# A two-layer hybrid block and two attention layers on one core: two weights of the next stage loaded into other pools, head norms in two halves

## The chip, the core and the metric

The kernel runs on one core of a Trainium2 chip. The metric is the device time of one execution in microseconds, as the median of several runs. TensorE does the matrix products, VectorE and ScalarE the elementwise work, GpSimd small steps on scale factors, and SyncE's queue issues the transfers from and to HBM.

## The reference, cut

512 tokens of 1024 channels, float32. A first block has two layers; each computes, with RMS norms over the channels:

```python
for l in range(DEPTH):                       # 2
    h = rms_norm(x, pre_mix_g[l]);  z = h @ w_in[l]
    mix = concat([o_a, o_b, o_c, o_d]) @ w_out[l]
    x = x + rms_norm(mix, post_mix_g[l])
    h = rms_norm(x, pre_ffn_g[l])
    y = conv_glu_ffn(h, ffn_w_gate[l], ffn_w_up[l], ffn_conv_w[l], ffn_w_down[l])
    x = x + rms_norm(y, post_ffn_g[l])
```

The four mixers of a layer, 256 channels each, are HGRN2 (a), gated linear attention (b), latent attention (c) and a gated delta net (d). In a, b and d each head of 64 channels of the output is RMS-normed and multiplied by a gate: these are the head norms. The FFN has 2816 inner channels. Behind this block come a layer A (differential attention) and a layer B (stick-breaking attention), both with attention to a memory of 256 rows, which the change doesn't touch in the source.

## The kernel before

**Products.** Float32 operands are split into a high and a low part of the type that TensorE takes (float32r), and a product is three matmuls: high by high, high by low, low by high (`mm3`). For a weight of 128 x 1024, `wload` (line 799) transfers it to a tile of pool "wr", ScalarE casts it into a tile of "wh" (the high part), and VectorE subtracts that from the original into a tile of "wl" (the low part). `preload` (790) does this ahead of need and keeps the result; the next `wload` of the same weight takes it. Pool "wr" has 2 tiles, "wh" and "wl" 4 each. The other large tiles (`p4`, 128 x 1024 or two halves) come from the pools "h" (8 tiles), "p" (8) and "w" (16). PSUM has the pools psA (3), psS (3) and psD (2).

**Stages.** Tokens go in four token tiles of 128. Each of the four stages of the first block (mixers 0, FFN 0, mixers 1, FFN 1) ends with `out_proj` (1829): 4 (mixers) or 11 (FFN) pairs of row blocks of the output weight, for two halves of 512 output channels. The last four pairs of the second half are held back, so that their products finish one token tile after another. For each tile, `residual_norm` (1793, the `done` in the code) squares the two halves (ScalarE), makes the scale (GpSimd: multiply and add, then a power), multiplies by it and by the gain (VectorE) and adds to the residual (VectorE); then `next_norm` (850) norms the tile for the next stage (square on ScalarE, scale on GpSimd, multiplication on VectorE), and `trans_split` (839) transposes it on TensorE and splits it into high (ScalarE) and low (VectorE) parts of h, two token tiles later. `rest()` transposes the last two tiles. `fm_first` (879) starts the next stage with three weights on the first 256 tokens, then calls `rest()`, then does the other 256. Only at the last token tile does `out_proj` call `preload(*then)` for the next stage's first weights. The squares and scaled halves stand in tiles of pool "p" behind the mixers and of "w" behind the FFN.

**Head norms.** `finish` (1044) norms the heads of the mixers a, b and d of each layer, six calls: square over 1024 columns (four token tiles of 256), sums over 64 columns, then the scale of 16 columns on GpSimd (`rstd`, 742: multiply and add, then a power), the multiplication by the gate, and that by the scale.

**Order.** Nothing is issued when it is written. The class `Plan` (262) records every operation, and all of them are issued by line 328. `feasible` (378) ranks them under the capacity of the pools, `simulate` (422) runs a list scheduler with its own costs over the five queues, and `order` (410) returns the order of the whole program. A change of one tile's pool or of one operation's size can so move any instruction of the program; each engine then takes its own queue strictly in order and waits at its head.

## Time and profile before

| | us |
|---|---|
| runs | 2032.98, 2035.56, 2035.82 |
| median | 2035.56 |
| the profiled execution's own time | 2033.99 |
| its span | 2032.2 |
| TensorE busy in it | 1954.1 (96%) |
| VectorE busy | 1250.3 (62%) |
| ScalarE busy | 946.6 (47%) |
| GpSimd busy | 265.7 (13%) |

The chain of work that ended last consists of TensorE for 84% of the span, VectorE for 7%, ScalarE for 3% and GpSimd for 2%. The stages can be told by what TensorE multiplies: mixers 0 until 325 us, a first seam until 376, FFN 0 until 710, a second seam until 745, mixers 1 until 1050, a third seam until 1100, FFN 1 until 1434, a fourth seam until 1475, layer A until 1740, layer B until the end. The table by stage shows where TensorE stands still, and the rows of single engines in the seams and in the mixers what it stands still for. As all operations are issued from one line, rows are told apart by their tiles: wr, wh and wl are a weight, its high and its low part; p4h is h; p4w and p4p are tiles of the pools "w" and "p"; st are small tiles with sums and scale factors.

### The profile page before, as it was taken

To read this page: it belongs to the slowest core of one execution; us is meant where nothing else is said; L and a number is where in the kernel's file an instruction comes from. 1 tells how busy PE (TensorE), PEld (TensorE's weight loads), DVE (VectorE), ACT (ScalarE), POOL (GpSimd) and SP (SyncE) were. 2 spreads that over 40 slices of the span, in tenths; PEclk is the share of its full clock that TensorE was granted. 3 is DMA by queue.
4 is the path that set the end of the run, shared out by engine and by line. 5 is a ranking of instruction groups with operands and counts; after the bars stand their busy time and mean duration, and the time that the engine had idled before them with its cause. 6 is when DMAs were issued, how large, how long until landed. Compare 5 with 4: busy or idle time off the path is not lost.

```text
span 2032.2 us, 33173 instructions
## 1 busy us (share of the span) xinstructions
PE 1954.1 (96%) x13254; PEld 1655.6 (81%) x13254; DVE 1250.3 (62%) x2319; ACT 946.6 (47%) x1715; POOL 265.7 (13%) x362
## 2 busy tenths in 40 slices
PE   7999989899999989998898999999999999999999
PEld 6888778788888878887787888888899988888787
DVE  7688873544442257878836444422548886558796
ACT  5744463433332236633634333322446774457782
POOL 3101111000000021011201000000223220005131
PEclk9999989999999999999999999999999999999999
DMA  5321224433332433302243333324331213421121
GB/s 166 97 63 36 83 81 138 125 94 94 98 99 94 155 90 96 92 24 68 82 152 112 100 94 94 99 97 167 121 89 43 84 63 114 135 84 55 60 74 62
DMA packets 231305, 191.62 MB, mean 94 GB/s; under 512 B 22352, under 2 KB 201200, under 8 KB 231152
## 3 DMA queue, kind: packets, MB, share of 16 engines
q1 hardware_dynamic: 231152, 189.51, 30.4%
q8 instruction: 104, 1.70, 0.3%
q14 instruction: 49, 0.40, 0.1%
HBM read 174.28 MB, written 15.20 MB: 93 GB/s over the span
## 4 chain that ended last, share of the span: by engine, by line
PE 84%; DVE 7%; ACT 3%; POOL 2%; issue 2%; DMA 1%; SPq 1%; DVEq 0%; ACTq 0%; POOLq 0%
PE psA L328 63%; PE psS L328 12%; PE psD L328 9%; DVE p4w L328 5%; POOL st L328 2%; ACT p4w L328 1%; DVE p4p L328 1%; DVE wl L328 1%; SPq L328 1%; DVE p L328 1%; ACT wh L328 0%; DMA wr<-in_w_in_dram 0%; ACT p4p L328 0%; ACT p L328 0%; DVE p4h L328 0%
## 5 line engine op out<-in xcount | busy, mean ns | idle before, releaser
L328 PE MATMUL psA<-p4h,wh 128*128 128x512 f32 (+1 forms) x2144 | 627.9, 377 | 14.3 <-DVE p4h L328 7.1
L328 DVE TENSOR_TENSOR wl<-wr,wh 128x1024 fp32r<-128x1024 f32 (+6 forms) x304 | 349.0, 1152 | 413.7 <-ACT wh L328 408.4
L328 ACT CAST wh<-wr 128x1024 fp32r<-128x1024 f32 (+6 forms) x304 | 298.5, 990 | 465.2 <-PE psA L328 279.8
L328 PEld LDWEIGHTS psA<-p4h,wh 128*128 128x128 f32 x2144 | 393.5, 191 | 89.9 <-DVE p4h L328 8.3
L328 PE MATMUL psA<-p4h,wl 128*128 128x512 f32 (+1 forms) x1072 | 400.6, 374 | 0.0
L328 PE MATMUL psA<-wh,p4h 128*128 128x256 f32 (+1 forms) x1792 | 353.8, 289 | 0.9 <-DVE p4h L328 0.7
L328 PEld LDWEIGHTS psA<-wh,p4h 128*128 128x128 f32 x1792 | 282.3, 188 | 6.6 <-issue 2.0
L328 PE MATMUL psA<-wl,p4h 128*128 128x256 f32 (+1 forms) x896 | 257.5, 288 | 0.4 <-DVE wl L328 0.4
L328 PEld LDWEIGHTS psA<-p4h,wl 128*128 128x128 f32 x1072 | 204.3, 191 | 37.0
L328 POOL TENSOR_SCALAR st<-st 128x1 f32<-128x1 f32 (+4 forms) x108 | 46.1, 427 | 1310.6 <-ACT p4w L328 908.5
L328 PEld LDWEIGHTS psA<-wl,p4h 128*128 128x128 f32 x896 | 168.8, 188 | 2.6 <-DVE wl L328 0.8
L328 PE MATMUL psA<-wh,p4w 128*128 128x512 f32 (+1 forms) x540 | 159.4, 368 | 0.0
L328 ACT ACTIVATE p<-p 128x512 f32<-128x512 f32 (+2 forms) x174 | 87.3, 526 | 100.2 <-DVE p L328 98.9
L328 POOL TENSOR_TENSOR st<-st,c 128x1 f32<-128x1 f32 (+4 forms) x106 | 115.4, 1090 | 8.0
L328 ACT ACTIVATE p4w<-psA 128x256 f32<-128x256 f32 (+5 forms) x138 | 61.6, 452 | 107.0 <-PE psA L328 105.9
L328 PEld LDWEIGHTS psA<-wh,p4w 128*128 128x128 f32 x540 | 96.6, 188 | 18.2 <-issue 0.5
L328 PE MATMUL psS<-consts,p4w 128*128 128x128 f32 (+1 forms) x448 | 70.5, 291 | 36.7 <-DVE p4w L328 28.9
L328 PE MATMUL psS<-p4w,p4w 128*64 128x64 f32 (+9 forms) x800 | 94.6, 271 | 5.3 <-DVE p4w L328 5.1
L328 PE MATMUL psA<-wl,p4w 128*128 128x512 f32 (+1 forms) x270 | 98.5, 365 | 0.0
L328 PE MATMUL psS<-wh,p4w 128*128 128x512 f32 x300 | 97.3, 395 | 0.0
L328 DVE TENSOR_TENSOR p<-psA,p 128x512 f32<-128x512 f32 x54 | 37.3, 691 | 95.8 <-PE psA L328 94.2
L328 PEld LDWEIGHTS psS<-consts,p4w 128*128 128x128 f32 x448 | 54.5, 153 | 47.7 <-issue 19.1
(227 smaller groups left out, 3105.0 us busy)
## 6 DMA issues: line engine op xcount, KB each, us to landing
wr<-in_w_in_dram SPq DMA_DIRECT2D x44, 512.0 KB, 3.8
wr<-in_ffn_w_gate_dram SPq DMA_DIRECT2D x44, 512.0 KB, 3.8
wr<-in_ffn_w_up_dram SPq DMA_DIRECT2D x44, 512.0 KB, 3.8
wr<-in_ffn_w_down_dram SPq DMA_DIRECT2D x44, 512.0 KB, 3.5
wr<-in_w_out_dram SPq DMA_DIRECT2D x16, 512.0 KB, 4.7
wr<-in_a_w_in_dram SPq DMA_DIRECT2D x16, 512.0 KB, 3.8
wr<-in_b_w_in_dram SPq DMA_DIRECT2D x16, 512.0 KB, 3.9
p4w<-xd SPq DMA_DIRECT2D x12, 512.0 KB, 4.4
```

The costliest lines, as they stand in the source:

```text
L328: op.fn(*op.args, **op.kw)
```

## The change

`out_proj` takes a string `early`. Ahead of the loop over the last products it preloads the first two weights of the next stage, the first into two tiles (high and low) of pool "p", the second into two of pool "w". All four callers give "pw". The weights that `then` names beyond these two are preloaded at the last token tile as before. `finish` does the sums, the scale and the two multiplications in two halves of 512 columns (two token tiles, 8 scale factors each). The unused argument `eng` goes.

```diff
@@ -787,16 +787,16 @@
         self.mm(ps, a, b[0], True, False)
         self.mm(ps, a, b[1], False, not more)
 
-    def preload(self, *views, eng=None):
+    def preload(self, *views, tag=None):
 
         for v in views:
             if self.wkey(v) not in self.ready_w:
-                self.ready_w[self.wkey(v)] = self.wload(v, eng)
+                self.ready_w[self.wkey(v)] = self.wload(v, tag)
 
     def wkey(self, view):
         return view.tensor.name, view.offset, tuple(view.shape)
 
-    def wload(self, view, eng=None):
+    def wload(self, view, tag=None):
 
         if self.wkey(view) in self.ready_w:
             return self.ready_w.pop(self.wkey(view))
@@ -805,10 +805,13 @@
         for k in range(sh[1] if len(sh) == 4 else 1):
             part = (slice(None), k) if len(sh) == 4 else slice(None)
             self.SP.dma_start(out=raw[part], in_=view[part])
-        hi = self.new(self.pwh, 4, sh, F32R, "wh", "wh")
-        lo = self.new(self.pwl, 4, sh, F32R, "wl", "wl")
+        if tag:
+            hi, lo = (self.p4(sh, F32R, tag) for _ in range(2))
+        else:
+            hi = self.new(self.pwh, 4, sh, F32R, "wh", "wh")
+            lo = self.new(self.pwl, 4, sh, F32R, "wl", "wl")
         self.A.copy(hi, raw)
-        self.sub(lo, raw, hi.bitcast(F32), eng)
+        self.sub(lo, raw, hi.bitcast(F32))
         return hi, lo
 
     def mm3(self, out, a, b, start, stop):
@@ -1044,15 +1047,18 @@
     def finish(self, o, gate, kt0, pst):
 
         sq = self.p4()
-        self.act(sq, o, AF.Square)
         ss = self.st([128, 16])
-        self.rsum(ss, sq.rearrange("p (a d) -> p a d", d=64))
+        parts = [(slice(i * 512, i * 512 + 512), slice(i * 8, i * 8 + 8)) for i in range(2)]
+        heads = lambda a: a.rearrange("p (a d) -> p a d", d=64)
+        for c, n in parts:
+            self.act(sq[:, c], o[:, c], AF.Square)
+            self.rsum(ss[:, n], heads(sq[:, c]))
         yield lambda: gate.get("done")
-        r = self.rstd(ss, 64)
-        self.mul(o, o, gate["gate"])
-        yield self.when(r)
-        ov = o.rearrange("p (a d) -> p a d", d=64)
-        self.mul(ov, ov, r.unsqueeze(2).broadcast_to([128, 16, 64]))
+        for c, n in parts:
+            r = self.rstd(ss[:, n], 64)
+            self.mul(o[:, c], o[:, c], gate["gate"][:, c])
+            yield self.when(r)
+            self.mul(heads(o[:, c]), heads(o[:, c]), r.unsqueeze(2).broadcast_to([128, 8, 64]))
         yield self.when(o)
         self.to_mixT(o.rearrange("p (t c) -> p t c", t=NT), kt0, pst, gate["gain"])
 
@@ -1826,7 +1832,7 @@
                 yield 0.0
         return views, gen
 
-    def out_proj(self, W, lhs, order, done, first, second, then):
+    def out_proj(self, W, lhs, order, done, first, second, then, early=""):
 
 
 
@@ -1853,6 +1859,8 @@
                 ps1 = [self.ps(p) for p in second]
             for t in range(NT):
                 part(ps0 if i < len(order) else ps1, t, n, w)
+        for v, tag in zip(then, early):
+            self.preload(v, tag=tag)
         for t in range(NT):
             if not late:
                 ps1[t] = self.ps(second[t])
@@ -1899,7 +1907,7 @@
         self.xt = self.load_x(acts[NF - 1][:, 0, :].bitcast(F32), "w")
         return self.out_proj(Wd, lambda k, t: (acts[k][:, 0, t * 128:(t + 1) * 128], acts[k][:, 1, t * 128:(t + 1) * 128]),
                              list(range(0, NF, 2)), lambda t, ps: self.residual_norm(t, ps, gb, "w"),
-                             "SSSD", "AAAD", then)
+                             "SSSD", "AAAD", then, "pw")
 
     def layer1(self, l, steps):
 
@@ -1923,7 +1931,7 @@
         self.xt = self.load_x(mt[3][:, 0, :].bitcast(F32), "p")
         steps = self.out_proj(Wo, lambda k, t: (mt[k][:, 0, t * 128:(t + 1) * 128], mt[k][:, 1, t * 128:(t + 1) * 128]),
                               order, lambda t, ps: self.residual_norm(t, ps, gb, "p"), "AAAD", "SSSD",
-                              self.ffn_views(l)[:3])
+                              self.ffn_views(l)[:3], "pw")
         if self.upto == f"mix{l}":
             return run(steps)
         h, rest = self.next_norm(steps, I["pre_ffn_g"][l], "h")
```

The order in which the instructions stand shows where the moved ones come to stand. VectorE at seam 1 (mixers 0 to FFN 0), from the low half of h of token tile 0 on, before. wl_767 and wl_770 are the first two weights of the FFN, p4w_758 the normed token tile 2, p4p_775 the scaled halves of tile 3, p4p_691 its residual, and the last row is the low half of h of tile 1:

```order
L328 TENSOR_TENSOR p4h_700<-psS_763,p4h_696 128x2x128
L328 TENSOR_TENSOR wl_767<-wr_765,wh_766 128x1024
L328 SCALAR_TENSOR_TENSOR p4w_758<-p4p_690,st_761,p4w_692 128x1024
L328 TENSOR_TENSOR wl_770<-wr_768,wh_769 128x1024
L328 SCALAR_TENSOR_TENSOR p4p_775<-psD_704,st_778,p4w_687 128x512
L328 SCALAR_TENSOR_TENSOR p4p_775<-psD_764,st_778,p4w_687 128x512
L328 TENSOR_TENSOR p4p_691<-p4p_691,p4p_775 128x512 x2
L328 TENSOR_TENSOR p4h_697<-psS_784,p4h_693 128x2x128
```

VectorE at the same place after the change. p4p_737 and p4w_740 are the low parts of the first two weights, wl_779 is that of the third, p4w_770 the normed tile 2, p4p_781 the scaled halves of tile 3, and p4h_703 ends the piece with the low half of tile 1. Its first part, at the residual of tile 0:

```order
L328 TENSOR_TENSOR wl_734<-wr_732,wh_733 128x1024
L328 TENSOR_TENSOR p4p_737<-wr_735,p4p_736 128x1024
L328 SCALAR_TENSOR_TENSOR p4p_743<-psA_707,st_746,p4w_693 128x512
L328 SCALAR_TENSOR_TENSOR p4p_743<-psS_741,st_746,p4w_693 128x512
L328 TENSOR_TENSOR p4w_740<-wr_738,p4w_739 128x1024
L328 TENSOR_TENSOR p4p_694<-p4p_694,p4p_743 128x512 x2
```

and VectorE in its second part, at the end of the seam:

```order
L328 TENSOR_TENSOR p4h_706<-psS_775,p4h_702 128x2x128
L328 TENSOR_TENSOR wl_779<-wr_777,wh_778 128x1024
L328 SCALAR_TENSOR_TENSOR p4w_770<-p4p_696,st_773,p4w_698 128x1024
L328 SCALAR_TENSOR_TENSOR p4p_781<-psD_710,st_784,p4w_693 128x512
L328 SCALAR_TENSOR_TENSOR p4p_781<-psD_776,st_784,p4w_693 128x512
L328 TENSOR_TENSOR p4p_697<-p4p_697,p4p_781 128x512 x2
L328 TENSOR_TENSOR p4h_703<-psS_790,p4h_699 128x2x128
```

The subtractions of the first two weights moved up to the residual of tile 0; that of the third stands where that of the first stood, and none stands between the norm of tile 2 and the residual of tile 3.

VectorE at seam 2 (FFN 0 to mixers 1) before, from the low half of tile 0 on. wl_1158 and wl_1161 are the first two weights of the mixers, p4w_1150 the normed tile 2, p4w_1163 the scaled halves of tile 3, p4w_1008 its residual, and p4h_1049 the low half of tile 1:

```order
L328 TENSOR_TENSOR p4h_1052<-psS_1155,p4h_1048 128x2x128
L328 TENSOR_TENSOR wl_1158<-wr_1156,wh_1157 128x1024
L328 TENSOR_TENSOR wl_1161<-wr_1159,wh_1160 128x1024
L328 SCALAR_TENSOR_TENSOR p4w_1150<-p4w_1007,st_1153,p4w_1044 128x1024
L328 SCALAR_TENSOR_TENSOR p4w_1163<-psD_1056,st_1166,p4w_1004 128x512
L328 SCALAR_TENSOR_TENSOR p4w_1163<-psD_1096,st_1166,p4w_1004 128x512
L328 TENSOR_TENSOR p4w_1008<-p4w_1008,p4w_1163 128x512 x2
L328 TENSOR_TENSOR p4h_1049<-psS_1172,p4h_1045 128x2x128
```

VectorE at seam 2 after the change. wl_1182 is the small weight of the mixers, cast and subtracted in pieces, wl_1196 the next full weight, p4w_1152 and p4w_1162 are the normed tiles 1 and 2, and p4h_1055 is the low half of tile 1:

```order
L328 TENSOR_TENSOR p4h_1058<-psS_1167,p4h_1054 128x2x128
L328 TENSOR_TENSOR wl_1182<-wr_1180,wh_1181 128x8x56
L328 TENSOR_TENSOR wl_1182<-wr_1180,wh_1181 128x8x8
L328 TENSOR_TENSOR wl_1182<-wr_1180,wh_1181 128x8x32
L328 TENSOR_TENSOR wl_1182<-wr_1180,wh_1181 128x8x16 x2
L328 TENSOR_TENSOR wl_1196<-wr_1194,wh_1195 128x1024
L328 SCALAR_TENSOR_TENSOR p4w_1152<-p4w_1012,st_1155,p4w_1050 128x1024
L328 SCALAR_TENSOR_TENSOR p4w_1162<-p4w_1013,st_1165,p4w_1050 128x1024
L328 SCALAR_TENSOR_TENSOR p4w_1169<-psD_1062,st_1172,p4w_1010 128x512
L328 SCALAR_TENSOR_TENSOR p4w_1169<-psD_1102,st_1172,p4w_1010 128x512
L328 TENSOR_TENSOR p4w_1014<-p4w_1014,p4w_1169 128x512 x2
L328 TENSOR_TENSOR p4h_1055<-psS_1178,p4h_1051 128x2x128
```

The two full subtractions left (they stand above, beside the residuals); the small weight and one full weight came in, and the norm of tile 1 moved down behind them.

VectorE at the tail of mixers 0 before. p4w_495 is the output of the last of the head-normed mixers, st_651 its scale of 16 columns; p4w_645 and p4w_658 are the normed rows of the memory attention:

```order
L328 TENSOR_TENSOR p4w_495<-p4w_495,p4p_289 128x1024
L328 TENSOR_SCALAR st_634<-st_633 128x1
L328 TENSOR_TENSOR p4w_495<-p4w_495,st_651 128x1024
L328 SCALAR_TENSOR_TENSOR p4w_645<-p4w_646,st_649,p4w_640 128x1024
L328 SCALAR_TENSOR_TENSOR p4w_658<-p4w_659,st_662,p4w_640 128x1024
```

VectorE there after the change (p4w_650 and p4w_664 are the memory rows, st_656 and st_661 the two scales of 8 columns):

```order
L328 SCALAR_TENSOR_TENSOR p4w_650<-p4w_651,st_654,p4w_645 128x1024
L328 TENSOR_SCALAR p_544_639<-p_544_639,st_640 128x512
L328 SCALAR_TENSOR_TENSOR p4w_664<-p4w_665,st_668,p4w_645 128x1024
L328 COPY p4w_632<-psD_657 128x2x128
L328 TENSOR_TENSOR p4w_495<-p4w_495,p4p_289 128x512 x2
L328 TENSOR_TENSOR p4w_495<-p4w_495,st_656 128x512
L328 TENSOR_TENSOR p4w_495<-p4w_495,st_661 128x512
```

The memory rows moved ahead of the multiplications by gate and scale, which now stand in halves.

## Rows read from the trace of the kernel before

**Rows 1.** Table by stage; columns: us, PE, PEld, DVE, ACT, POOL busy (xcount), PEclk, DMA, GB/s.

```profile
0.00:325.00 325.00, 296.21 (x2968) 253.00 (x2969) 245.80 (x519) 170.42 (x310) 52.84 (x69) 0.98 0.33 97
325.00:376.00 51.00, 43.86 (x231) 36.91 (x230) 27.12 (x40) 20.34 (x46) 11.18 (x20) 0.93 0.32 107
376.00:710.00 334.00, 334.00 (x1485) 273.60 (x1486) 137.21 (x159) 107.65 (x135) 0.58 (x3) 1.00 0.35 106
710.00:745.00 35.00, 28.09 (x129) 22.68 (x128) 21.23 (x34) 15.38 (x37) 11.15 (x19) 0.91 0.31 98
...
1434.00:1475.00 41.00, 39.65 (x237) 33.94 (x237) 28.74 (x45) 19.45 (x44) 12.64 (x25) 1.00 0.35 116
```

**Rows 2.** TensorE's timeline at seam 1: start, us, engine, line, op, [idle before <-releaser].

```profile
357.05 0.51 PE L328 MATMUL psA<-p4h,wh 128*128 128x256 f32 x2 [0.64 <-ACT p4h L328]
359.59 0.63 PE L328 MATMUL psS<-consts,p4w 128*128 128x128 f32 x4 [2.04 <-DVE p4w L328]
363.49 0.58 PE L328 MATMUL psA<-p4h,wh 128*128 128x256 f32 x1 [3.27 <-DVE p4h L328]
```

**Rows 3.** VectorE's timeline at seam 1.

```profile
350.62 1.30 DVE L328 SCALAR_TENSOR_TENSOR p4w<-p4p,st,p4w 128x1024 f32<-128x1024 f32 x1 [2.19 <-POOL st L328]
...
356.21 1.21 DVE L328 TENSOR_TENSOR wl<-wr,wh 128x1024 fp32r<-128x1024 f32 x1
358.15 1.30 DVE L328 SCALAR_TENSOR_TENSOR p4w<-p4p,st,p4w 128x1024 f32<-128x1024 f32 x1 [0.72 <-POOL st L328]
359.37 1.21 DVE L328 TENSOR_TENSOR wl<-wr,wh 128x1024 fp32r<-128x1024 f32 x1
360.50 1.40 DVE L328 SCALAR_TENSOR_TENSOR p4p<-psD,st,p4w 128x512 f32<-128x512 f32 x2
...
363.02 0.74 DVE L328 TENSOR_TENSOR p4h<-psS,p4h 128x256 fp32r<-128x256 f32 x2
```

**Rows 4.** GpSimd's timeline at seam 1.

```profile
349.75 0.19 POOL L328 TENSOR_SCALAR st<-st 128x1 f32<-128x1 f32 x1 [3.97 <-ACT p4w L328]
...
356.24 1.24 POOL L328 TENSOR_SCALAR st<-st 128x1 f32<-128x1 f32 x1 [3.91 <-ACT p4w L328]
```

**Rows 5.** TensorE's timeline at seam 2.

```profile
739.79 1.08 PE L328 MATMUL psS<-consts,p4w 128*128 128x128 f32 x4 [3.65 <-DVE p4w L328]
742.91 0.80 PE L328 MATMUL psA<-p4h,wh 128*128 128x256 f32 x2 [2.04 <-ACT wh L328]
```

**Rows 6.** Timeline of VectorE and GpSimd at seam 2.

```profile
734.29 2.35 DVE L328 TENSOR_TENSOR wl<-wr,wh 128x1024 fp32r<-128x1024 f32 x2
734.38 2.39 POOL L328 TENSOR_SCALAR st<-st,st 128x1 f32<-128x1 f32 x1 [3.42 <-ACT p4w L328]
...
738.36 1.28 DVE L328 SCALAR_TENSOR_TENSOR p4w<-p4w,st,p4w 128x1024 f32<-128x1024 f32 x1 [1.72 <-POOL st L328]
```

**Rows 7.** TensorE's timeline at seam 4.

```profile
1465.50 0.50 PE L328 MATMUL psA<-wh,p4h 128*128 128x256 f32 x2 [0.75 <-DVE p4h L328]
```

**Rows 8.** Timeline of the start: GpSimd, VectorE, TensorE.

```profile
10.21 0.56 POOL L328 TENSOR_TENSOR st<-st,c 128x1 f32<-128x1 f32 x1
...
11.00 1.23 DVE L328 TENSOR_TENSOR wl<-wr,wh 128x1024 fp32r<-128x1024 f32 x1 [2.62 <-ACT wh L328]
...
13.47 1.12 PE L328 MATMUL psS<-consts,p4w 128*128 128x128 f32 x4 [3.08 <-DVE p4w L328]
```

**Rows 9.** VectorE's timeline at the tail of mixers 0.

```profile
286.30 1.29 DVE L328 SCALAR_TENSOR_TENSOR p4w<-p4w,st,p4w 128x1024 f32<-128x1024 f32 x1 [0.73 <-POOL st L328]
```

**Rows 10.** Groups by line and form, whole span: xcount, busy us, mean ns, idle before.

```profile
L328 DVE TENSOR_TENSOR p4w<-p4w,p4p 128x1024 f32<-128x1024 f32 x10 | 12.2, 1217 | 0.0
...
L328 DVE TENSOR_TENSOR p4w<-p4w,p4w 128x512 f32<-128x512 f32 x16 | 10.3, 682 | 0.0
...
L328 POOL TENSOR_TENSOR st<-st,c 128x16 f32<-128x16 f32 x10 | 32.9, 3285 | 0.8
...
L328 POOL TENSOR_TENSOR st<-st,c 128x8 f32<-128x8 f32 x12 | 21.9, 1827 | 1.0
```

## The prediction

> **What bounds the kernel now.** I read the table by stage first [rows 1]. TensorE is busy for 334.00 of the 334 us of the first FFN stage and for 296.21 of the mixers' 325 us, at a granted clock of 1.00 and 0.98: there the time is TensorE's own work, and the change takes no product away. The seams between the stages are the exception. Seam 1 (first mixers to first FFN, 325 to 376 us) leaves TensorE idle for 51.00 - 43.86 = 7.1 us at a clock of 0.93, seam 2 (first FFN to second mixers, 710 to 745 us) for 35.00 - 28.09 = 6.9 us at 0.91, seam 3 (second mixers to second FFN) repeats seam 1, and seam 4 (second FFN to layer A) for only 41.00 - 39.65 = 1.35 us at 1.00. So some 7.1 + 6.9 + 7 + 1.35 = 22 us of the 2032 are idle in the four places that the change speaks of.
>
> Then TensorE's own rows at seam 1 [rows 2]: it waits 0.64, 2.04 and 3.27 us, and the longest wait ends when VectorE has written the low half of h for token tile 1; products run without a gap only from 363.49. Why that half is late stands in VectorE's rows [rows 3]: a weight's subtraction (1.21 us from 356.21), the norm of token tile 2 (from 358.15, after 0.72 us of waiting for GpSimd), another subtraction (1.21 us from 359.37), two residual products and two additions, and only then, at 363.02, the split that TensorE needs. GpSimd's rows [rows 4] tell why the norm waits: its scale step ends late because a step on 128x1, which took 0.19 us at 349.75, took 1.24 from 356.24, while VectorE's subtraction ran.
>
> Seam 2 shows it larger [rows 5, 6]: TensorE waits 3.65 and 2.04 us; two subtractions run for 2.35 us from 734.29, and GpSimd's step on 128x1 takes 2.39 us beside them. The norm that TensorE waits for starts at 738.36. Seam 4 is nearly full already: the longest wait there is 0.75 us [rows 7].
>
> **Part 1, the two early weights.** No instruction is added: two loads, two casts and two subtractions of a seam go earlier, into tiles of other pools. What counts is what stands ahead of the split in VectorE's queue afterwards, and the change's order tells that. At seam 1 the two subtractions go up beside the residuals of token tiles 0 and 1, where VectorE has gaps (2.19 us ahead of 350.62, while from 358.15 on it has none) [rows 3]. But the third weight's subtraction takes the place of the first ahead of the norm of tile 2, and the split of tile 1 still stands behind that norm and behind the residual of tile 3. So one subtraction slot leaves: 1.21 us as a row, about 1.13 as the distance to the next start (359.37 to 360.50). Against it, the two weight tiles take two of the pool "p" slots in which the residuals' squares are made, so that the square of tile 2 waits for an earlier addition; I charge 0.1 us. Gain 1.0 us at seam 1, and 1.0 at seam 3, whose waits are the same. Bounds of each: a loss of 0.5 (the moved subtractions push the additions ahead of the squares by part of their 1.21) to a gain of 2.4 (the slot, plus GpSimd's step back from 1.24 to 0.19, which frees the norm by 1.05, and some of the wait behind it).
>
> A page of the Trainium skill, "SBUF — State Buffer", section "Who interferes with whom", says that a VectorE instruction with two SBUF inputs and a GpSimd instruction that reads SBUF exclude each other for a whole instruction. The traces agree: the step of 128x1 lasts as long as the two subtractions beside it [rows 6]. By the page alone, taking both subtractions out of the place would give the whole GpSimd stretch back (rival B); by the order, another subtraction stands in the same place, and the sum keeps 1.0.
>
> At seam 2 the two subtractions (2.35 us) leave as well, but in the change's order the small-weight subtractions (five of them) and one of the next full weight now stand ahead of the norms of tiles 1 and 2; the norm of tile 1 stood ahead before. 2.35 - 1.21 for the full weight [rows 3] leaves 1.1; for the small ones, of which the trace of before shows none in this place, I take 0.3, between nothing and the 1.2 of a full weight, nearer to nothing since they hold 448 of 1024 columns. That is 0.8, with bounds of a loss of 1.5 (the third weight's load lands late and both norms wait behind it) and a gain of 2.5. At seam 4 no more than the 1.3 us of idle time can go; I take 0.5 (0 to 1.3). The seams give 1.0 + 1.0 + 0.8 + 0.5 = 3.3 us.
>
> **Part 2, the head norms in halves.** In each of six places a full pass over 1024 columns becomes two over 512: the multiply by the gate 1217 to 2 x 682 ns, the multiply by the scale and the sum likewise [rows 10]. That is 0.15 us more for each of the three, 0.45 on VectorE; on GpSimd the power of 16 columns at 3285 ns becomes two of 8 at 1827, so 0.37 us more. ScalarE's square becomes two as well; ScalarE is busy for 170.42 of the 325 us [rows 1], and I charge nothing. The first half of the scale factors is ready about 1.5 us sooner, the second 0.4 later. These norms stand in the mixers, where TensorE has other products to run (296.21 of 325 busy), so I cost them at nothing where they stand as before; without that cover they cost 6 x (0.45 + 0.37) = 4.9 us, which is rival D.
>
> A page of the Trainium skill, "VectorE: DVE Perf Modes", section "The TRN2 errata — SBUF-src ops pay a fixed extra latency per instruction", speaks against this part: each instruction pays a fixed extra cost, many small tiles pay it each. The rows agree, 2 x 682 against 1217 ns. By the page's 58 cycles at 0.96 GHz it would be an estimated 0.06 us per instruction more, by the rows 0.15; the rows decide.
>
> **What moves with it.** The scheduler lays out the whole program anew, so three other places change. At the start, the norm of token tile 1 now goes ahead of the first weight's subtraction on VectorE; before, the subtraction ran from 11.00 for 1.23 us and the norm behind it, and TensorE waited 3.08 us for that norm until 13.47 [rows 8]. Its scale is ready when GpSimd's power ends, at 10.21 + 0.56 = 10.77, so that the norm can start near 10.9, 1.2 sooner. The next wait, for the h of tile 0 and its weight, then ends later by the same subtraction: I take 0.8 of gain (0 to 1.3). At the tail of the mixers the norms of the memory rows stood behind the two multiplies of the last head norm (1.2 us each, as the group of the first says [rows 10]) and then waited 0.73 us each for GpSimd (one of the two waits is in [rows 9]); they now stand ahead of the halves. The two 0.73 can go and nothing else by it, half of it at both tails: 0.75 each, 1.5 in all (bounds: a loss of 1, since the head norm's transposes come later, to a gain of 3 each). Everywhere else I take zero, and 5 us either way as a bound: the first mixers leave TensorE idle for 325 - 296.21 = 28.8 us, start included [rows 1], the second for about half of that, and a new order may shift a ninth of the sum.
>
> **The sum.** 3.3 + 0.8 + 1.5 = 5.6 us off. The profiled execution took 2033.99 us (span 2032.2 and 1.8 around it): 2028.4. The median of three runs is 2035.56, 1.6 above the profiled one, so on its scale 2030.0. A change of 0.2% is 4.1 us, about what a measurement of this kernel tells from none: faster is below 2031.5, slower above 2039.6.
>
> **The rivals.** B, the seams give all: neither the third weight's subtraction nor the small ones collide with GpSimd, so that each of seams 1 to 3 gives 2.4 us (2.35 at seam 2 [rows 6], the upper bound above at the others). 7.2 + 0.5 + 0.8 + 1.5 = 10.0: about 2025.6. For it speak the rows of GpSimd [rows 4, 6]; against it the order, in which another subtraction takes the place. 0.20. C, the seams give nothing: the split of tile 1 still stands behind the norm of tile 2 and the residual of tile 3 in VectorE's queue, and the chain from the last product through the square, GpSimd and the residual is as long as before; the saved slot is then only waiting. With the start's 0.8 alone: 2034.8. For it speaks that the split stands where it stood; against, that VectorE was busy without a gap from 358.15 to 363.02, with the subtraction among it [rows 3]. 0.21. D, slower: the head norms' halves lie on the path. VectorE takes its queue in order; where the second half's scale ends last and the multiply by it stands ahead of work that TensorE waits for, each of six places costs 0.45 + 0.37 = 0.82, and 4.9 with nothing gained at the seams gives 2035.6 + 4.9 = 2040.5. It decides where the second multiply stands within some 2 us of the first, less than GpSimd's 1827 ns and its first step behind one another. For it: all three multiplies stand in one row in the change's order; against: TensorE has other work in most of those places. The reshuffle's 5 us of loss would end there too. 0.17. A, the forecast, 0.42.
>
> **How the numbers follow.** A reaches over 2026 to 2034, B over 2022 to 2028, C over 2032 to 2038, D from 2039.6 on. Leaving out most of D and the last of B, 2022 to 2040 holds 8 in 10. Faster by over 0.2%: all of B and seven tenths of A, 0.50. Within: the rest of A and C, 0.33. Slower: 0.17.
>
> **What would show it.** Seam 1's products without a gap from about 362.4 instead of 363.49 after the last output product, and seam 2's from a time 0.8 earlier against its last output product: Part 1 holds. A step on 128x1 of GpSimd at 0.2 us in both seams, and a norm of tile 2 a microsecond sooner: B. The same distance as before from the last output product to the first dense one: C. Waits of VectorE for GpSimd ahead of the second halves, with TensorE waiting for VectorE behind them: D. A mixer stage that takes 3 us more or less than 325 or 305 would say that the new order outside the seams counts for more than all of these, and that would make the prediction wrong in its reasons even where the time is right.

## The result, and the profile after

The changed kernel takes 2025.28 us (median of five runs, 2023.03 to 2030.09) against 2035.82 (five runs, 2032.98 to 2037.69): a ratio of 0.9950, with a 95% interval of 0.9933 to 0.9967. In a second comparison (the run after_again below) the ratio was 0.9933 (0.9919 to 0.9946). One of the 29 runs of before in it took 2162.66 us at a granted clock of 0.843 and is left out of the ratio. So it is faster by 10 to 14 us; 2030.0 was forecast, with 2022 to 2040 as the range. The time came out on that of rival B (2025.6), but not by B's mechanism.

The profiled execution of the changed kernel took 2030.09 us (span 2027.9), the slowest of its five runs. Its table by stage, with the columns and the cuts of [rows 1]:

```profile
0.00:325.00 325.00, 296.27 (x2954) 254.91 (x2955) 246.03 (x528) 168.73 (x312) 52.67 (x73) 0.96 0.32 94
325.00:376.00 51.00, 46.04 (x237) 39.09 (x236) 28.80 (x39) 20.47 (x43) 9.17 (x20) 0.93 0.41 133
376.00:710.00 334.00, 333.63 (x1488) 273.59 (x1487) 136.37 (x160) 107.11 (x138) 0.58 (x3) 1.00 0.33 103
710.00:745.00 35.00, 31.11 (x139) 25.17 (x138) 23.73 (x40) 17.64 (x39) 9.72 (x17) 0.91 0.47 142
...
1434.00:1475.00 41.00, 41.00 (x264) 36.86 (x263) 28.15 (x43) 18.67 (x44) 15.85 (x29) 1.00 0.45 142
```

TensorE is busier in the seams (46.04 of 51 us instead of 43.86, 31.11 of 35 instead of 28.09, all of 41 instead of 39.65), but the cuts of before fall at other places of the work here. A closer measure is the distance from the last output product of a seam to the first product of the next stage behind which TensorE stands still no more. TensorE's timeline at seam 1, of before and then of after; the last output product is the first row of each:

```profile
354.13 0.40 PE L328 MATMUL psD<-wh,p4w 128*128 128x512 f32 x1
...
355.78 0.63 PE L328 MATMUL psS<-consts,p4w 128*128 128x128 f32 x4 [0.81 <-DVE p4h L328]
```

```profile
357.46 0.40 PE L328 MATMUL psD<-wh,p4w 128*128 128x512 f32 x1
...
359.11 0.39 PE L328 MATMUL psA<-p4h,p4p 128*128 128x256 f32 x1 [0.38 <-ACT p4h L328]
...
361.64 0.63 PE L328 MATMUL psS<-consts,p4w 128*128 128x128 f32 x4 [1.91 <-DVE p4w L328]
364.94 1.43 PE L328 MATMUL psA<-p4h,p4p 128*128 128x256 f32 x5 [2.67 <-DVE p4h L328]
```

Before it is 363.49 [rows 2] - 354.13 = 9.36 us, after 364.94 - 357.46 = 7.48. The waits are 0.38, 1.91 and 2.67 us, where [rows 2] have 0.64, 2.04 and 3.27, and the one of 0.81 went. Here are the same distances and the pieces between them for the profiled executions that the argument goes by (us; each is worked out from two such rows; "rest" runs from the last product of FFN 1 to the end of the span):

| kernel | mixers 0 | seam 1 | FFN 0 | seam 2 | mixers 1 | seam 3 | FFN 1 | rest | span |
|---|---|---|---|---|---|---|---|---|---|
| before | 354.1 | 9.36 | 369.7 | 9.77 | 335.1 | 9.29 | 369.6 | 575.3 | 2032.2 |
| before_again | 353.1 | 9.36 | 369.4 | 9.79 | 337.7 | 9.29 | 369.8 | 575.8 | 2034.3 |
| after | 357.5 | 7.48 | 370.2 | 5.96 | 335.9 | 7.48 | 370.5 | 573.0 | 2027.9 |
| after_again | 350.8 | 7.48 | 369.9 | 5.96 | 332.2 | 7.48 | 370.4 | 573.3 | 2017.4 |
| early_only | 358.1 | 7.47 | 370.5 | 7.81 | 335.5 | 7.53 | 370.0 | 573.6 | 2030.5 |
| halves_only | 351.5 | 9.33 | 370.8 | 9.78 | 337.8 | 9.32 | 370.5 | 576.1 | 2035.0 |
| halves_again | 350.4 | 9.35 | 370.8 | 9.79 | 336.7 | 9.36 | 369.5 | 574.7 | 2030.5 |
| squares_first | 354.1 | 7.68 | 370.4 | 9.64 | 336.2 | 7.67 | 370.3 | 581.0 | 2037.0 |
| no_low_parts | 353.2 | 8.22 | 370.2 | 6.36 | 335.5 | 8.15 | 370.2 | 576.1 | 2027.8 |

Two things are to be read in it. The seams repeat to 0.04 us between two executions of one kernel, so one profile is enough for them. The mixers do not: they differ by 6.7 us (357.5 and 350.8) between two executions of the changed kernel alone.

One thing the table hides: the distance ends where TensorE stands still no more, and how much it has multiplied by then differs from kernel to kernel. Counted in the same timelines to the start of the tenth product of the next stage, ahead of which every kernel here has done the same twelve transposes, the distances are (us):

| kernel | seam 1 | seam 2 | seam 3 |
|---|---|---|---|
| before, before_again | 11.02, 11.02 | 11.43, 11.45 | 10.95, 10.95 |
| after, after_again | 8.92, 8.93 | 9.26, 9.26 | 8.93, 8.93 |
| early_only | 8.91 | 9.26 | 8.98 |
| halves_only, halves_again | 10.99, 11.02 | 11.43, 11.45 | 10.98, 11.02 |
| squares_first | 9.34 | 11.31 | 9.33 |
| no_low_parts | 9.67 | 7.52 | 9.60 |

By equal work the seams gave 2.1, 2.2 and 2.0 us, 6.3 in all. At seam 2 the first table shows 3.8, because in the changed kernel the gapless stretch begins with less work done.

The mean of the two executions after less that of the two before is 2022.65 - 2033.25 = -10.6 us; by the pieces of the first table: the three seams -7.5, the rest (seam 4 with layers A and B) -2.4, mixers 1 -2.4, mixers 0 +0.5, and the FFNs +1.2. That last goes with the clock. At seam 1, in the 3 us behind the first 3 us of gapless products the granted clock was 0.93 before and 0.67 after, so a part of the idle time that TensorE saved was spent again at 1.2 GHz.

```profile
366.50:369.50 3.00, 3.00 (x26) 3.00 (x26) 2.20 (x4) 0.00 (x0) 0.00 (x0) 0.93 0.55 161
```

```profile
367.90:370.90 3.00, 3.00 (x19) 3.00 (x19) 2.40 (x3) 0.00 (x0) 0.00 (x0) 0.67 0.09 24
```

### The profile page after: what moved, and what is told of

It is laid out like the page before. It is cut to its first block, busy times and chain, and to the rows that moved or that the text cites. A ratio compares the mean times of both kernels' runs of the same rounds, so it can differ in the third digit from the quotient of the medians.

```text
span 2027.9 us, 33217 instructions
## 1 busy us (share of the span) xinstructions
PE 1959.3 (97%) x13254; PEld 1664.9 (82%) x13254; DVE 1252.7 (62%) x2337; ACT 943.5 (47%) x1719; POOL 261.0 (13%) x374
## 4 chain that ended last, share of the span: by engine, by line
PE 82%; DVE 8%; ACT 2%; issue 2%; DMA 2%; POOL 2%; SPq 1%; DVEq 0%; ACTq 0%; POOLq 0%
PE psA L328 62%; PE psS L328 12%; PE psD L328 9%; DVE p4w L328 5%; POOL st L328 2%; ACT p4w L328 1%; DVE p4p L328 1%; DVE st L328 1%; DVE wl L328 1%; SPq L328 1%; DVE p L328 1%; DMA dn<-p4w 1%; ACT wh L328 0%; DVE p4h L328 0%; DMA p4p<-in_x_dram 0%
## 5 line engine op out<-in xcount | busy, mean ns | idle before, releaser
L328 DVE TENSOR_TENSOR wl<-wr,wh 128x1024 fp32r<-128x1024 f32 (+4 forms) x296 | 339.4, 1151 | 413.3 <-ACT wh L328 408.1
L328 PE MATMUL psA<-p4h,wh 128*128 128x512 f32 (+1 forms) x1952 | 588.5, 384 | 0.0
L328 ACT CAST wh<-wr 128x1024 fp32r<-128x1024 f32 (+4 forms) x296 | 290.0, 989 | 480.3 <-PE psA L328 285.4
L328 PEld LDWEIGHTS psA<-p4h,wh 128*128 128x128 f32 x1952 | 362.5, 190 | 76.4 <-issue 2.5
L328 PE MATMUL psA<-p4h,wl 128*128 128x512 f32 (+1 forms) x976 | 376.2, 386 | 0.0
L328 PE MATMUL psA<-wh,p4h 128*128 128x256 f32 (+1 forms) x1728 | 345.9, 291 | 0.0
L328 PEld LDWEIGHTS psA<-wh,p4h 128*128 128x128 f32 x1728 | 275.2, 189 | 4.9 <-issue 2.0
L328 PE MATMUL psA<-wl,p4h 128*128 128x256 f32 (+1 forms) x864 | 249.9, 290 | 0.0
L328 PEld LDWEIGHTS psA<-p4h,wl 128*128 128x128 f32 x976 | 185.7, 190 | 33.1
L328 POOL TENSOR_SCALAR st<-st 128x1 f32<-128x1 f32 (+4 forms) x114 | 39.7, 348 | 1274.0 <-ACT p4w L328 872.4
```

The source lines that it names most:

```text
L328: op.fn(*op.args, **op.kw)
```

## The experiments

My theory after the first profile: the seams give the gain, each by its own queue. Rivals: the halves and the order that they bring give it; or any new order of the whole program does.

**The two parts apart.** after_again is the changed kernel itself. early_only has `finish` as before; halves_only has `out_proj` and its callers as before; early_mix_only is early_only with one caller fewer:

```diff
-                             "SSSD", "AAAD", then, "pw")
+                             "SSSD", "AAAD", then)
```

> The changed kernel once more, for a second profile. Its five runs reached from 2023.0 to 2030.1 us and the profiled one was the slowest of them. Theory (the seams give the gain): the distance from the last output product to the first gapless product of the next stage is again 7.5 us at seams 1 and 3 (before 9.4 and 9.3) and about 6 at seam 2 (before 9.8), whatever the run's time; the median lies at 2023 to 2028. Rival (the new order inside the mixers gives the gain and the seams little): the end of the first mixers' output products, at 357.5 us in the first profile against 354.1 before, moves ahead of 354 in a run of 2025 or less.

> The early weights alone, the head norms whole as before. Theory (seams): 1.9 + 3.8 + 1.8 us at seams 1 to 3, some 1 to 2 at the start and at seam 4, so 8 to 10 off: 2026 to 2028. Rival (the halves and the order that they bring give it): 2 to 4 off, 2032 to 2034.

> The head norms in halves alone, all weights of the next stage preloaded at the last token tile as before. Theory (seams): no change or a small one, 2033 to 2037, with the distances at the seams as before (9.4, 9.8, 9.3). Rival (halves give the gain): 2026 to 2030. Rival D of the prediction (the halves lie on the path): 2039 to 2041.

> The early weights only where the mixers end (seams 1 and 3), not where the FFNs end; the head norms whole. Theory (each seam gives its own part): 1.9 + 1.8 us at the two seams and what the start gives, so 3.5 to 5 off: 2031 to 2032.5, the distance at seam 2 as before (9.8). Rival (the order of the whole program gives the gain): a time that has nothing to do with the two seams, off by over 3 us from this.

All four were compared with the same runs of before (median 2036.75). after_again: 2022.59, ratio 0.9933 (0.9919 to 0.9946). early_only: 2033.15, ratio 0.9984 (0.9976 to 0.9993). halves_only: 2033.05, ratio 0.9988 (0.9976 to 0.9999). early_mix_only: 2032.81, ratio 0.9982 (0.9969 to 0.9995). So each part alone is worth 0.1 to 0.2%, and both together 0.7%: more than the sum of the two. The seams belong to the early weights alone (early_only has 7.47, 7.81, 7.53; halves_only 9.33, 9.78, 9.32; by the tenth product early_only has all of the changed kernel's gain at each seam), as the theory says; but early_only missed the 2026 to 2028 expected of it, and halves_only, at 2033.05, lies at the edge of "no change". Where the rest of the gain comes from is told below, with the clock.

early_mix_only (2031 to 2032.5 expected, so a little above) shows 7.48 at seam 1 and, as expected, 9.77 at seam 2, where nothing is early; but at seam 3, 10.56 us instead of 7.5. That seam is told below, with w_after_ffn.

**What shortened seams 1 and 3.** The prediction had put it down to a subtraction slot that leaves VectorE's queue. The trace of after doesn't bear this out. ScalarE's timeline at seam 1, before:

```profile
348.52 1.06 ACT L328 ACTIVATE p4w<-p4p 128x1024 f32<-128x1024 f32 x1 [4.88 <-DVE p4p L328]
...
349.57 0.58 ACT L328 ACTIVATE p4p<-psS 128x512 f32<-128x512 f32 x1
```

and after:

```profile
351.42 0.60 ACT L328 ACTIVATE p4p<-psS 128x512 f32<-128x512 f32 x1 [0.54 <-PE psS L328]
...
352.01 1.05 ACT L328 ACTIVATE p4w<-p4p 128x1024 f32<-128x1024 f32 x1
```

The square over 128x512 from psS is that of the residual of token tile 2, the square over 128x1024 the norm square of tile 1. Before, the first stands behind the second, which waits 4.88 us for VectorE; after, it stands ahead. Two rows of VectorE are swapped with them: the norm of tile 1 stood ahead of the scaled halves of tile 2 (350.62 [rows 3], then 352.36) and now stands behind them (354.55, behind 353.22). GpSimd's power for these halves ran beside that norm before and doesn't any more. GpSimd before, and after:

```profile
350.93 1.40 POOL L328 TENSOR_TENSOR st<-st,c 128x1 f32<-128x1 f32 x1
```

```profile
352.63 0.55 POOL L328 TENSOR_TENSOR st<-st,c 128x1 f32<-128x1 f32 x1
```

Counted from the last output product, VectorE began the norm of tile 2 at 358.15 [rows 3] - 354.13 = 4.02 us before and at 360.20 - 357.46 = 2.74 after. VectorE at seam 1 after, from the last subtraction ahead of the split:

```profile
358.27 1.22 DVE L328 TENSOR_TENSOR wl<-wr,wh 128x1024 fp32r<-128x1024 f32 x1
360.20 1.29 DVE L328 SCALAR_TENSOR_TENSOR p4w<-p4p,st,p4w 128x1024 f32<-128x1024 f32 x1 [0.72 <-POOL st L328]
361.94 1.41 DVE L328 SCALAR_TENSOR_TENSOR p4p<-psD,st,p4w 128x512 f32<-128x512 f32 x2 [0.45 <-POOL st L328]
...
364.47 2.07 DVE L328 TENSOR_TENSOR p4h<-psS,p4h 128x256 fp32r<-128x256 f32 x6
```

From the start of that norm to the start of the split it took 363.02 - 358.15 = 4.87 us before [rows 3] and 364.47 - 360.20 = 4.27 after: the slot of 1.21 us left, but 0.45 us of waiting for GpSimd came in ahead of the residual's products (361.94). So 1.28 us of the 1.88 lie ahead of the norm, and 0.60 in the queue behind it. Two kernels tell the two causes apart. squares_first adds a rule for the scheduler's order of squares and nothing else in the source (the scheduler then moves rows of VectorE with them, as in the changed kernel):

```diff
+        if t in (1, 2):
+            sq, norm = self.plan.ops[-1], self.norm_sq[t - 1]
+            norm.preds.append(sq.n)
+            sq.succs.append(norm.n)
```

no_low_parts leaves out what the prediction had charged:

```diff
+        if self.skip_lo:
+            return hi, hi
         self.sub(lo, raw, hi.bitcast(F32), eng)
```

> The kernel before with one rule more for the scheduler: ScalarE squares the residual of token tiles 1 and 2 ahead of the norm square of the tile before (as it stands in the changed kernel); all weights as before, head norms whole. Theory (the order on ScalarE carries most of what the seams gave: the residual of tile 2 was 2.5 us and the norm of tile 2 1.28 us nearer to the last output product): the distance at seams 1 and 3 falls from 9.36 and 9.29 us to about 8.1. Rival (the subtraction slots that leave VectorE's queue carry it): it stays at 9.3 or falls by less than 0.3.

> The kernel before with the subtractions of the first two weights at each seam left out (their high part stands for the low part in the products, so this part of the computation is left out); the place of the loads is as before. Theory of the prediction (slots in VectorE's queue and GpSimd's step beside them): the distance at seam 1 falls by 1.0 to 2.4 us, to 7.0 to 8.4, and GpSimd's step on 128x1 is back at 0.2 us. Rival (the order on ScalarE carries all): less than 0.6 us, 8.8 or more.

squares_first: 7.68 and 7.67 us at seams 1 and 3, so the order that starts with ScalarE's squares gives 1.68 and 1.62 of the 1.88 and 1.81, more than expected, with both subtractions where they were. The swap on ScalarE and the one on VectorE came together and are not told apart by it. Its time is nevertheless above before: 2041.78, ratio 1.0022 (1.0006 to 1.0038). The 3.3 us gained came back in layers A and B (581.0 instead of 575.3 and 575.8), whose order the scheduler had changed too. TensorE's idle time there is 14.6 us instead of 12.6 and 12.7, so waits are 2.0 of the 5.5 us, and what lengthened the rest is not shown. One of the waits, for ScalarE:

```profile
1549.18 0.73 PE L328 MATMUL psS<-p4p,p4p 128*128 128x512 f32 x2 [1.54 <-ACT p L328]
```

no_low_parts (2029.54 us in its one run): 8.22 and 8.15, so the subtractions in the place of before are worth 1.14 us, as the theory of the prediction had it (1.0 to 2.4), and GpSimd's step is back at 0.19 us. The third weight's subtraction moved up in it, between the residual's products (1.22 us at 358.52), so 1.14 is what the two gave with that one added. The two causes overlap: 1.68 + 1.14 is more than 1.88. In the changed kernel the step is not back:

```profile
358.30 1.24 POOL L328 TENSOR_SCALAR st<-st 128x1 f32<-128x1 f32 x1 [4.20 <-ACT p4w L328]
```

It takes the 1.24 us of [rows 4] still, since the third weight's subtraction runs beside it (1.22 us from 358.27). So B's mechanism didn't occur at seam 1. At seam 2 no_low_parts fell from 9.77 to 6.36, that is by 3.4 us (3.9 by the tenth product): there the subtractions weigh most.

**Seam 2.** The changed kernel has 5.96 there, early_only 7.81, before 9.77; by the tenth product 9.26, 9.26 and 11.43. TensorE before (the last output product and the transposes behind it), then TensorE, VectorE and GpSimd after:

```profile
733.14 0.40 PE L328 MATMUL psD<-wh,p4p 128*128 128x512 f32 x1
733.38 1.04 PE L328 MATMUL psS<-consts,p4w 128*128 128x128 f32 x8
```

```profile
735.09 0.40 PE L328 MATMUL psD<-wh,p4p 128*128 128x512 f32 x1
738.17 1.68 PE L328 MATMUL psS<-consts,p4w 128*128 128x128 f32 x8 [2.68 <-DVE p4w L328]
741.05 0.58 PE L328 MATMUL psA<-p4h,p4p 128*128 128x256 f32 x1 [1.20 <-ACT p4h L328]
...
742.90 4.08 PE L328 MATMUL psA<-p4h,p4p 128*128 128x256 f32 x23
```

```profile
734.30 2.62 DVE L328 TENSOR_TENSOR wl<-wr,wh 128x448 fp32r<-128x448 f32 x6
736.84 1.27 DVE L328 SCALAR_TENSOR_TENSOR p4w<-p4w,st,p4w 128x1024 f32<-128x1024 f32 x1
738.71 1.28 DVE L328 SCALAR_TENSOR_TENSOR p4w<-p4w,st,p4w 128x1024 f32<-128x1024 f32 x1 [0.59 <-POOL st L328]
```

```profile
735.41 0.23 POOL L328 TENSOR_SCALAR st<-st 128x1 f32<-128x1 f32 x1
736.31 1.85 POOL L328 TENSOR_SCALAR st<-st,st 128x1 f32<-128x1 f32 x1 [0.68 <-ACT p4w L328]
```

Six subtractions (five pieces of the small weight, 1.41 us together, and a full one) take 2.62 us in the place where two full ones took 2.35 [rows 6], and GpSimd's step for the residual of tile 3 is again stretched (1.85 us). So VectorE's queue got no shorter there, and the norm of tile 1, now behind the subtractions, holds eight transposes up until 738.17 that before ran at 733.38, right behind the output products. What came sooner is the norm of tile 2: it starts 738.71 - 735.09 = 3.62 us behind the last output product, where before it was 738.36 [rows 6] - 733.14 = 5.22. GpSimd's first step for it (735.41, 0.23 us) now stands ahead of the stretched one, where before both its steps stood behind the 2.39 us of [rows 6]. And the last wait of before, 2.04 us for ScalarE's cast of a weight [rows 5], is gone, since the casts stand early now. How much each of the two gives was not tried.

The halves don't deepen this seam. early_only, TensorE:

```profile
736.07 0.40 PE L328 MATMUL psD<-wh,p4p 128*128 128x512 f32 x1
...
743.88 4.29 PE L328 MATMUL psA<-p4h,p4p 128*128 128x256 f32 x23 [0.48 <-DVE p4h L328]
```

The run of 23 products, behind twelve transposes and three products in both kernels, begins 743.88 - 736.07 = 7.81 us behind the last output product in early_only and 742.90 - 735.09 = 7.81 in the changed kernel. In early_only a wait of 0.48 us stands right ahead of that run, so that its gapless stretch begins there; in the changed kernel none does, and the stretch begins at 741.05 already. That is all of the difference between 7.81 and 5.96.

**Other tiles for the early weights.** three_early gives "www" for all four callers (three early weights where the mixers end); w_after_ffn keeps "pw" there and gives "ww" where the FFNs end. Without any tag, in the pools "wh" and "wl", the early call leaves every instruction of the program in its old place: it is the other pools, not the earlier call, that move the weights.

> The changed kernel with three early weights at seams 1 and 3, and all early weights in pool w. VectorE then subtracts a weight ahead of the split of tile 0 instead of beside GpSimd's scale of the norm of tile 2. Theory (GpSimd's step is stretched by the subtraction beside it): its step goes from 1.24 us back to 0.2, the distance at seams 1 and 3 from 7.5 to 6.5 to 6.9, the time 1 to 2 us below the changed kernel's. Rival (the split waits for the residual of tile 3 whatever GpSimd does): 7.3 to 7.6, no change.

> The changed kernel with both early weights in pool w where the FFNs end (seams 2 and 4) and in p and w where the mixers end (seams 1 and 3), since three_early, which had pool w everywhere, left only 1.6 us at seam 2. Theory (each seam follows from its own tiles): 7.5 us at seams 1 and 3 as in the changed kernel, 1.6 to 3 at seam 2 instead of 6.0, and a time 2 to 4 us below the changed kernel's. Rival (the order of the whole program shifts more than the seams give): seam 2 falls but the time is the changed kernel's or above.

three_early: 2023.59, ratio 0.9916 (0.9894 to 0.9938), not to be told from the changed kernel. At seam 1 it missed both expectations: GpSimd's step takes 1.99 us, since now the second of two norms and then a subtraction run beside it, and the distance is 8.11, with 20 transposes inside it instead of 12. TensorE's waits in it sum to 3.83 us, though, against 4.96 in the changed kernel: the distance holds more work, not more waiting.

```profile
352.85 1.99 POOL L328 TENSOR_SCALAR st<-st 128x1 f32<-128x1 f32 x1 [1.79 <-ACT p4w L328]
```

At seam 2 it shows 1.61 us to the first gapless stretch, with later waits of 0.52 and 0.77 inside the mixers (the tenth product at 4.35 instead of 9.26). w_after_ffn took over that seam 2 (1.62) but came to 2025.87, ratio 0.9958 (0.9946 to 0.9971): the rival. At seam 3 it lost what seam 2 gave (tenth product at 14.29 instead of 8.93, against 4.36 instead of 9.26). TensorE's timeline at seam 3 of w_after_ffn:

```profile
1071.62 1.97 PE L328 MATMUL psS<-consts,p4w 128*128 128x128 f32 x8 [3.89 <-DVE p4w L328]
...
1079.84 0.69 PE L328 MATMUL psS<-consts,p4w 128*128 128x128 f32 x2 [5.61 <-DVE p4w L328]
```

ScalarE and GpSimd there:

```profile
1061.78 0.60 ACT L328 ACTIVATE p4p<-psA 128x512 f32<-128x512 f32 x1 [5.25 <-DMA xd<-p4p]
```

```profile
1055.47 0.52 POOL L328 MEMSET p4p<- 64x512 f32 x1 [3.90 <-DVE p4p L328]
```

The square of the residual of tile 1 waits 5.25 us, until a store of the residual has left a tile of pool "p". Two early weight tiles are in that pool, and here GpSimd has also cleared a tile of it for a later layer at 1055.47. In early_mix_only the same square waits 4.04 us for the same store, and the same clearing stands ahead of it (1060.80); this is its 10.56 us:

```profile
1065.90 0.60 ACT L328 ACTIVATE p4p<-psA 128x512 f32<-128x512 f32 x1 [4.04 <-DMA xd<-p4p]
```

In the changed kernel the clearing stands elsewhere, at seam 4. That the clearing and the early tiles together leave no tile free is read from these rows; a kernel without the clearing was not run. The cost of the early tiles that I had put at 0.1 us is thus nothing or several us, as the order has it.

**What the halves do.** halves_last_norm has them only in the head norm of gated linear attention; other_order changes one of the scheduler's own costs and nothing else; before_again and halves_again are second profiles.

```diff
-                return 0.3 + 0.165 * _free(op.outs[0])
+                return 0.3 + 0.19 * _free(op.outs[0])
```

> The kernel before with one cost of the scheduler changed (its own estimate for a power on GpSimd, 0.165 to 0.19 us per column): the same instructions in another order. Rival (a new order alone moves the mixers by several us, so that the halves' gain is luck of the order): the time moves by over 3 us either way while the seams stay at 9.4, 9.8 and 9.3. Theory (the halves do it): within 2 us of the kernel before.

> The kernel before with halves only in the head norm of gated linear attention, the one that stands at the tail of the mixers. Theory (the halves' gain is the tail, where TensorE waits 1.1 + 3.3 + 0.9 + 0.7 us before): idle at the tail of each mixers' stage falls from 6.1 to 4.3 us or less, and the time is that of halves_only, 2 to 4 us below before. Rival (the halves of the other two norms give it): the tail and the time stay as before.

> The kernel before once more, for a second profile. The seams are 9.4, 9.8 and 9.3 us again. If the mixers' length swings from run to run by the clock alone, the idle time in them is again 14 to 16 us per stage while the busy time differs by up to some us from 325.6 and 319.6.

> The halves alone once more, for a second profile: idle time of the mixers as in the first (14.1 after the start, and 16.4 us), the tail at 4.3 and 4.1 us, the seams as before. If the first profile's longer FFN stages and layers (1.1, 0.9 and 0.7 us over before) belong to the kernel, they are there again; if to the run, not.

other_order: 2038.22, ratio 1.0000 (0.9987 to 1.0014): this other order alone gives nothing. halves_last_norm: 2039.74, ratio 1.0020 (1.0010 to 1.0030), slower, with waits of 1.15, 1.33, 0.81 and 1.92 us at the tail of mixers 0; so the halves of one norm don't do it, and the expectation failed. The second profiles (2036.1 and 2032.35 us) settle what varies. Idle time of TensorE in mixers 0 behind the start is 14.4 and 13.3 us before, 14.1 and 13.6 with the halves, 15.1 and 14.6 in the changed kernel: the halves save no idle time in sum. At the tail the four waits of before (1.14, 3.31, 0.92, 0.72) became one:

```profile
292.25 0.66 PE L328 MATMUL psS<-consts,p4w 128*128 128x128 f32 x2 [4.28 <-DVE p4w L328]
```

but others came in elsewhere (3.18 us at 203, for one). What differs is the clock. A stretch of 25 us at the tail of mixers 0, columns as in [rows 1], of before, halves_only, after_again and early_only:

```profile
278.00:303.00 25.00, 18.82 (x114) 14.34 (x113) 17.12 (x32) 15.71 (x27) 4.79 (x6) 0.80 0.21 68
```

```profile
278.00:303.00 25.00, 20.61 (x154) 17.36 (x153) 20.24 (x42) 16.45 (x31) 4.48 (x6) 0.93 0.36 120
```

```profile
277.00:302.00 25.00, 20.64 (x153) 17.30 (x152) 19.65 (x40) 16.32 (x31) 4.21 (x6) 0.93 0.34 118
```

```profile
283.00:308.00 25.00, 18.89 (x117) 14.48 (x116) 17.20 (x33) 15.95 (x28) 4.79 (x6) 0.80 0.25 80
```

With the halves TensorE is busy for 20.61 of 25 us at a granted clock of 0.93, without them for 18.82 at 0.80. In the first profile of the changed kernel the clock of the same stretch is 0.86, so the waits alone don't fix it:

```profile
282.00:307.00 25.00, 20.71 (x141) 16.72 (x141) 18.32 (x40) 15.69 (x31) 4.21 (x6) 0.86 0.27 94
```

Over a whole mixers' stage, cut into pieces of 4 us, the granted clock adds up to these times at the lower level of 1.2 GHz (twice the piece times what the clock lacks to 1), in us:

| | mixers 0 | mixers 1 |
|---|---|---|
| before, before_again | 13.6, 13.7 | 17.0, 23.9 |
| halves_only, halves_again | 6.9, 6.8 | 13.8, 13.6 |
| early_only | 23.9 | 23.9 |
| after, after_again | 23.9, 10.2 | 13.6, 6.9 |

A us at the lower level does about half a us of work (in the trace of before, two products of 256 columns take 0.43 us from start to start at 364.08, at the lower level, and 0.23 at 747.37). So early_only lost some (23.9 - 13.7) / 2 = 5 us in mixers 0, near the 358.1 against 353.6 us of the table above; the halves save about 3.4 us there by the clock; and the changed kernel, with both, has in one execution the one and in another the other. In mixers 1 the halves show no such gain (337.8 and 336.7 us against 335.1 and 337.7).

These are one or two executions each. The mean granted clock is on record for every run, and with it the parts can be added up: a run loses about its span times what its mean clock lacks to 1. That is an estimate, too high where TensorE waits at the lower clock, and a clock of 0.001 more or less is 2 us of a single run, so only the means over the runs that were compared together are given:

| kernel | runs | time, us | clock | lost, us | left, us |
|---|---|---|---|---|---|
| before | 28 | 2036.9 | 0.9858 | 28.9 | 2008.1 |
| early_only | 12 | 2033.6 | 0.9832 | 34.0 | 1999.5 |
| halves_only | 12 | 2034.3 | 0.9863 | 27.8 | 2006.5 |
| after_again | 6 | 2023.2 | 0.9878 | 24.6 | 1998.7 |

In what is left, the early weights give 8.6 us, the halves 1.6 and both 9.4: the parts add up, and the early weights have nearly all of it, as much as the theory expected of them (8 to 10). By the clock early_only then lost 5.1 us against before, and the changed kernel won 4.3. That explains why the times of the parts don't add up. The 0.2% by which halves_last_norm is slower is the clock's too (0.9846 against 0.9865 for before; left 2007.7 against 2007.4). And one kernel alone shows it: of the six runs of three_early two took 2012.85 and 2015.04 us at a clock of 0.994, the others 2022.83 to 2025.04 at 0.988 to 0.990. What decides in which kernel, and in which of its executions, the clock falls more often stays open: the waits in the two executions of the changed kernel are nearly the same ones.

## Why the prediction was right, and where not

**What bounds the kernel: right.** FFN 0 and FFN 1 stayed at 369 to 371 us in every kernel; the seams were the place.

**Part 1, seams 1 and 3: right in sign, too small, and mostly by another cause.** Forecast 1.0 each, measured 1.88 and 1.81 (2.1 and 2.0 by the tenth product). The step that failed is "so one subtraction slot leaves ... about 1.13": the slot gave 0.60 net, because the residual's products of tile 3 then waited 0.45 us for GpSimd, and the larger part (1.28) came ahead of the norm, from the swap on ScalarE and VectorE, which squares_first shows to be worth 1.6 to 1.7 alone. I had read VectorE's and GpSimd's queue in the order of instructions, and not ScalarE's, in which two rows are swapped. And the scarcer tiles of pool "p", which may be the occasion of the swap (not tried), I had named only as a cost of 0.1.

**Seam 2: right in sign, by the wrong terms.** Forecast 0.8 within a loss of 1.5 to a gain of 2.5. By equal work it is 2.2, inside the bounds, and the early weights alone give all of it; the distance of the first table fell by 3.8. The term that failed is the 0.3 for the small weight: the 448 columns that I gave its five pieces are those of the largest piece alone. In the change's order they hold 8 x (56 + 8 + 32 + 16 + 16) = 1024 columns, and they took 1.41 us. With that my working would have given 2.35 - 1.21 - 1.41, a loss of 0.3: the subtractions of the place took 2.62 us instead of 2.35, and nothing was gained by them. What gained, the norm of tile 2 that starts 1.6 us sooner and the wait for ScalarE's cast that went, I had not costed.

**Seam 4: mis-sized.** Forecast 0.5 (0 to 1.3). TensorE's idle time in the 25 us behind FFN 1's last product was 1.35 and 1.40 us and is nothing now (41.00 of 41 us busy in the table by stage), so 1.4, at the upper bound. The piece from there to the end fell by 2.4 us, its idle time by 1.7 (12.6 and 12.7 to 11.1 and 11.0): in layers A and B 0.3 us of waiting went, and the other 0.7 is not waiting and stays open.

**Part 2, the head norms: the costs right, the tail wrong.** The pieces cost what the rows of before said (685 ns for 512 columns, 1790 ns for a power over 8), and no 4.9 us appeared: rival D fell. The groups of after:

```profile
L328 DVE TENSOR_TENSOR p4w<-p4w,p4p 128x512 f32<-128x512 f32 x24 | 16.0, 685 | 4.0 <-ACT p4w L328 3.9
```

```profile
L328 POOL TENSOR_TENSOR st<-st,c 128x8 f32<-128x8 f32 x24 | 43.0, 1790 | 2.0
```

The step "the two 0.73 can go and nothing else by it" failed as a sum of waits: the waits of the tail fell from 6.1 to 4.3 us in mixers 0 and to 2.3 in mixers 1 (1.71 and 0.58), but the two 0.73 did not go: in the changed kernel VectorE still waits 0.65 and 0.45 us for GpSimd ahead of these norms (290.82 and 292.95). And idle time in the stage as a whole did not fall; the gain that is there is the clock's, which I had not costed at all.

**The start: right.** Idle time before the products run was 14.1 and 14.7 us before and 13.6 and 13.8 after, 0.7 on the mean, against 0.8 forecast. The norm of tile 1 frees TensorE at 11.62 instead of 13.47 [rows 8], and shorter waits follow.

**The rivals.** B's time, not its mechanism: at seam 1 the norm of tile 2 came 1.28 us sooner, as one of B's signs says, but GpSimd's step stayed at 1.24 us, against the other, and at 1.85 at seam 2. C and D fell: the distances shrank, and the halves cost nothing that shows. "5 us either way" for the new order was fair: squares_first lost 5.5 us in the rest, and the mixers moved by that much.

**The last sign.** A mixers' stage 3 us longer or shorter would make the reasons wrong even where the time is right, says the prediction. Read from one execution it came out: mixers 0 took 357.5 us against 354.1. But the second execution of the same kernel took 350.8, so no single one can be read that way. What counts outside the seams is the clock, some 4 of the 14 us of the second comparison.

So the time lies in the range in part by luck. Seams, seam 4 and start should have been 6.3 + 1.4 + 0.7 = 8.4 us instead of the 4.1 that the sum has for them, with all the terms of the seams too small; the tail's 1.5 did not come in the way that was forecast; and what the clock gave on top stood in no term.

## What to carry to other kernels

Where a scheduler orders a program anew, read the order of every engine on the chain, the one that only squares and copies too: the swap of two squares on ScalarE, with the two rows of VectorE that went with it, gave 1.6 to 1.7 us per seam at seams 1 and 3, more than leaving out the subtractions that the change was about (1.1). A tile taken early from a shared pool costs what the next user of that pool waits for, which can be nothing or 5 us, and stands in no duration. And where two executions of one kernel differ by 10 us, compare the pieces that repeat (the seams here, to 0.04 us), count them to the same piece of work on both sides, and take the others from several profiles or from the granted clock of every run.

## What was not expected of the hardware

The granted clock differed between two executions of one program by as much as the change was worth: 23.9 and 10.2 us at 1.2 GHz in mixers 0 of the changed kernel, with spans of 2027.9 and 2017.4 us. Four short waits in a row at the tail of the mixers went with a clock of 0.80 over 25 us, one longer wait of 4.28 us with 0.93 or, in another execution, 0.86. A step of GpSimd on a single column took 0.19 to 2.39 us by what VectorE did beside it (1.24 beside one subtraction of 1.21, 2.39 beside two of 2.35); with the subtraction gone it was 0.19. The Trainium skill, "SBUF — State Buffer", section "Who interferes with whom", says that a VectorE instruction with two SBUF inputs contends with a GpSimd instruction that reads SBUF; these rows agree.
